# Block inversion of a chunked RWKV-7 layer: its six phases write into the spare half of the chain's bank

## Chip, cores and metric

One Trainium2 chip, one core. The metric is the time of one execution in microseconds of device time; it is given as the median of the runs shown. The profile is of one further execution, taken by the hardware profiler.

## What is computed

Two layers of a decoder on 256 tokens of width 2048 in float32: an RWKV-7 time mixing layer and a differential attention layer, each followed by a gated MLP and layer norms. Only the first layer matters here. Its core is a recurrence over tokens with a 64 x 64 state for each of 32 heads:

```python
def step(S, inp):
    r_t, w_t, k_t, v_t, a_t, b_t = inp
    sa = jnp.einsum('bhij,bhj->bhi', S, a_t)
    S = S * w_t[:, :, None, :] + sa[..., None] * b_t[:, :, None, :] + v_t[..., None] * k_t[:, :, None, :]
    y = jnp.einsum('bhij,bhj->bhi', S, r_t)
    return S, y
...
y = ((y - mean) * lax.rsqrt(var + GN_EPS)).reshape(B, T, D) * lnx_g + lnx_b
...
return (y * g) @ w_o, v_first
```

## The kernel before

Every weight matrix is streamed from HBM, split by ScalarE (`hi`, line 217) and VectorE (`lo`, line 220) into two parts and multiplied in three products; these are the matmuls of lines 230 to 235 into tiles `psd`. They make up most of the kernel.

The recurrence is done in chunks of 64 tokens. The 32 heads are worked in eight groups of four heads (`NG` = 8). `pipeline` (line 1055, in the functions printed below) runs stages i = -3 to 7, and in each stage it traces several generators side by side, by a pace for each: the chain and the outputs of group i, the inversion (`lanes`) of group i + 1, the factors, corners and bonus of group i + 2, the dense products for r and k of group i + 3, and in the last three stages instead of these the first part of the output projection (`early`). The framework then makes each engine's order from this trace, with its own estimate of durations: an instruction that isn't ready is passed by later ones. It also puts in all the waits.

`lanes` inverts, for each of 16 blocks, a triangular 64 x 64 matrix in six phases. A phase is 64 matmuls of 32 x 32 (in the last two 32) into one PSUM tile, then an eviction by VectorE or ScalarE; the next phase needs the evicted values. The matmuls are at lines 1288, 1298, 1311, 1319, 1331 and 1341. The first phase starts from `W1`, which `corners` loads from DRAM, and from its transpose on VectorE (line 1280); the third starts from a transpose of line 1304. In the kernel before each phase takes a new tile from `pst()`: a pool of two banks (`pss`), which the phases share in rotation with the factors (line 1196, evicted into `M` at line 1199), the corners' transposes (line 1255), the bonus and the outputs.

`chain` goes through four chunks. It takes one bank `us` (a pool of one). First all four quarters of it get V centred (line 1374), which is copied into `UV`. From then on only the lower half of the bank is used: `up` (columns 0 to 127, line 1421) and `sp` (columns 128 to 255, line 1434). A chunk is: `rb` (lines 1394 and 1407, other banks), copies into `R`, `up`, copies into `UV` (ScalarE and VectorE), `sp`, the state `Sn` (VectorE, lines 1439 and 1440), and the outputs `yps` (lines 1411 and 1444, other bank). `outputs` normalizes `yps` and writes `V`; from group 4 on `z_parts` splits that into `S1` (lines 197 and 198), which `early` and the output projection multiply with.

The trace order of the chain's 13 steps and the six phases follows from their paces (37.24 and 18.62 with a start at 0.04): phase 1 stands ahead of `up` of chunk 0; phase 2 behind `sp` of chunk 0; phase 3 between `up` and `sp` of chunk 1; phase 4 ahead of `up` of chunk 2; phase 5 behind `sp` of chunk 2; phase 6 behind `up` of chunk 3.

Of the kernel before, what the change touches and what calls it, by code (L numbers as in the profile page):

```python
# [15 lines left out]
T = 256  # L16
# [983 lines left out]
class Groups:  # L1000
# [236 lines left out]
    def corners(self, g):  # L1237
# [31 lines left out]
                                  in_=self.dram(d2, par * 8, ((C, 32), (4 * DBL, 8), (1, 32)), at=be * 2 * DBL))  # L1269
        yield  # L1270

    def lanes(self, g):

        t, nc, g1 = self.t, self.nc, self.g1
        s = self.st[g]
        M, W1, Z = s["M"], s["W1"], self.Z
        rows = [slice(32 * q, 32 * q + 32) for q in range(4)]
        N = [self.units(M, 1)] * 2 + [self.units(M, 0)] * 2
        T0 = g1.tile([P, 8, 32], F32, name="T1")
        nc.vector.transpose(out=T0.rearrange("p u t -> p (u t)"), in_=W1.rearrange("p u t -> p (u t)"))  # L1280
        T0v, W1v = (x.rearrange("p u (b k i) -> p u b k i", b=2, k=2) for x in (T0, W1))
        ps = self.pst()
        pv = ps[:, :P].rearrange("p (u b i) -> p u b i", b=2, i=8)
        with self.ride():
            for u in range(8):
                for q, r in enumerate(rows):
                    be = 32 * (q % 2)
                    nc.tensor.matmul(pv[r, u], lhsT=N[q][r, u, be:be + 32], rhs=T0v[r, u, :, 0, :], start=True, stop=True)
        nc.vector.tensor_tensor(out=self.Z8[:, :, :, 0, :], in0=pv,
                                in1=t.x("m8", 16).rearrange("p (b i) -> p b i", b=2).unsqueeze(1).broadcast_to([P, 8, 2, 8]),  # L1290
                                op=ALU.mult)
        yield
        ps = self.pst()
        pv = ps[:, :P].rearrange("p (u b i) -> p u b i", b=2, i=8)
        with self.ride():
            for u in range(8):
                for r in rows:
                    nc.tensor.matmul(pv[r, u], lhsT=self.Z8[r, u].rearrange("p b k i -> p (b k i)"),
                                     rhs=W1v[r, u, :, 1, :], start=True, stop=True)
        nc.scalar.copy(out=W1v[:, :, :, 1, :], in_=pv)  # L1300
        yield

        T1 = g1.tile([P, 8, 32], F32, name="T1")
        nc.vector.transpose(out=T1.rearrange("p u t -> p (u t)"), in_=W1.rearrange("p u t -> p (u t)"))
        ps = self.pst()
        pv = ps[:, :P].rearrange("p (u t) -> p u t", t=16)
        with self.ride():
            for u in range(8):
                for q, r in enumerate(rows):
                    be = 32 * (q % 2)  # L1310
                    nc.tensor.matmul(pv[r, u, :], lhsT=N[q][r, u, be:be + 32], rhs=T1[r, u, :16], start=True, stop=True)
        self.copy(PACE["ez"][0], Z[:, :, :16], pv)
        yield
        ps = self.pst()
        pv = ps[:, :P].rearrange("p (u t) -> p u t", t=16)
        with self.ride():
            for u in range(8):
                for r in rows:
                    nc.tensor.matmul(pv[r, u, :], lhsT=Z[r, u, :], rhs=W1[r, u, 16:], start=True, stop=True)
        self.copy(PACE["ez"][1], W1[:, :, 16:], pv)  # L1320
        yield

        T2 = g1.tile([P, 8, 32], F32, name="T1")
        nc.vector.transpose(out=T2.rearrange("p u t -> p (u t)"), in_=W1.rearrange("p u t -> p (u t)"))
        Z2 = g1.tile([P, 8, 32], F32, name="T1")
        ps = self.pst()
        pv = ps[:, :T].rearrange("p (u t) -> p u t", t=32)
        with self.ride():
            for u in range(8):
                for q in (0, 2):  # L1330
                    nc.tensor.matmul(pv[rows[q + 1], u, :], lhsT=N[q][rows[q], u, 32:C], rhs=T2[rows[q], u, :],
                                     start=True, stop=True)
        nc.scalar.copy(out=Z2[rows[1]], in_=pv[rows[1]])
        nc.vector.tensor_copy(out=Z2[rows[3]], in_=pv[rows[3]])
        yield
        ps = self.pst()
        pv = ps[:, :T].rearrange("p (u t) -> p u t", t=32)
        with self.ride():
            for u in range(8):
                for q in (0, 2):  # L1340
                    nc.tensor.matmul(pv[rows[q], u, :], lhsT=Z2[rows[q + 1], u, :], rhs=W1[rows[q + 1], u, :],
                                     start=True, stop=True)
        for q in range(4):
            be = 32 * (q % 2)
            o = N[q][rows[q], :, be:be + 32]
            self.copy(PACE["wc"][q], o, W1[rows[q]])
        nc.scalar.copy(out=N[0][rows[0], :, 32:C], in_=pv[rows[0]])
        nc.vector.tensor_copy(out=N[2][rows[2], :, 32:C], in_=pv[rows[2]])
        yield
# [13 lines left out]
    def chain(self, g):  # L1363
# [3 lines left out]
        s = self.st[g]  # L1367
        AR, M, KBT, pc, UV, R = s["AR"], s["M"], s["KBT"], s["pc"], self.UV, self.R
        yps = s["y"] = self.psc.tile([P, GT, T], F32, name="yps")
        us = self.bank("us")  # L1370

        for jj in range(GT):
            for w in range(2):
# [173 lines left out]
```

## Time and profile before

| | us |
|---|---|
| median of the runs | 2480.97 |
| lowest and highest of 3 | 2474.71, 2485.47 |
| the profiled execution | 2477.43 |
| its span in the profile | 2475.7 |
| TensorE busy in the span | 2427.9 (98%) |
| VectorE busy | 1865.6 (75%) |
| ScalarE busy | 1516.3 (61%) |
| mean granted TensorE clock | 0.994 |

A busy engine is one with an instruction in flight, so 98% for TensorE doesn't say that it works at its peak. The stages of `pipeline` lie between about 145 and 560 us of the span; all that follows is attention and MLP, which the change doesn't touch. In the stages the idle time of TensorE, by who released it, tells what the order of the work costs, and the granted clock tells how long a matmul takes.

### The profile page before, as it was taken

To read this page: it belongs to the slowest core of one execution; us is meant where nothing else is said; L and a number is where in the kernel's file an instruction comes from. 1 tells how busy PE (TensorE), PEld (TensorE's weight loads), DVE (VectorE), ACT (ScalarE), POOL (GpSimd) and SP (SyncE) were. 2 spreads that over 40 slices of the span, in tenths; PEclk is the share of its full clock that TensorE was granted. 3 is DMA by queue.
4 is the path that set the end of the run, shared out by engine and by line. 5 is a ranking of instruction groups with operands and counts; after the bars stand their busy time and mean duration, and the time that the engine had idled before them with its cause. 6 is when DMAs were issued, how large, how long until landed. Compare 5 with 4: busy or idle time off the path is not lost.

```text
span 2475.7 us, 53133 instructions
## 1 busy us (share of the span) xinstructions
PE 2427.9 (98%) x18618; PEld 2160.6 (87%) x18618; DVE 1865.6 (75%) x4218; ACT 1516.3 (61%) x3447; POOL 144.5 (6%) x204
## 2 busy tenths in 40 slices
PE   8999999999999999999999999999999999999997
PEld 7988888877988888888889899988988888888886
DVE  8977788868977777776666867678987777776665
ACT  7756675646766666655555756656766666665554
POOL 0010000002200000001111000003200000001111
PEclk9999999999999999999999999999999999999999
DMA  7544443435566666667665555556566666666663
GB/s 244 186 129 120 116 114 115 135 102 159 161 201 188 192 188 190 188 191 226 188 187 160 182 173 166 177 172 181 168 202 190 190 189 189 189 191 184 190 188 121
DMA packets 276717, 428.49 MB, mean 173 GB/s; under 512 B 60632, under 2 KB 83168, under 8 KB 276448
## 3 DMA queue, kind: packets, MB, share of 16 engines
q1 hardware_dynamic: 276448, 425.10, 58.1%
q8 instruction: 145, 2.38, 0.4%
q14 instruction: 124, 1.02, 0.2%
HBM read 420.25 MB, written 6.31 MB: 172 GB/s over the span
## 4 chain that ended last, share of the span: by engine, by line
PE 87%; DVE 6%; ACT 3%; DMA 2%; issue 1%; SPq 0%; POOL 0%; ACTq 0%; DVEq 0%; POOLq 0%
PE psd L234 44%; PE psd L235 22%; PE psd L230 3%; PE psd L232 3%; PE psd L231 3%; DVE lo L220 2%; PE psd L285 1%; PE psd L283 1%; PE psd L284 1%; DMA raw<-in_rkv 1%; PE psd L937 1%; PE psd L936 1%; PE psd L938 1%; ACT hi L217 1%; PE lnst L348 1%
## 5 line engine op out<-in xcount | busy, mean ns | idle before, releaser
L217 ACT CAST hi<-raw 128x256 fp32r<-128x256 f32 (+3 forms) x2236 | 1079.0, 489 | 757.0 <-PE psd L234 542.6
L220 DVE TENSOR_TENSOR lo<-raw,hi 128x256 fp32r<-128x256 f32 (+3 forms) x2236 | 1150.3, 540 | 490.6 <-ACT hi L217 440.2
L234 PE MATMUL psd<-S,hi 128*128 128x512 f32 x2976 | 1040.2, 394 | 0.4 <-ACT hi L217 0.2
L235 PE MATMUL psd<-S,lo 128*128 128x256 f32 x2976 | 832.2, 280 | 0.3 <-DVE lo L220 0.2
L234 PEld LDWEIGHTS psd<-S,hi 128*128 128x128 f32 x2976 | 559.2, 188 | 128.1 <-ACT hi L217 1.0
L235 PEld LDWEIGHTS psd<-S,lo 128*128 128x128 f32 x2976 | 559.2, 188 | 1.7 <-DVE lo L220 1.5
L234 PE MATMUL psd<-hs,hi 128*128 128x512 f32 x1290 | 451.9, 395 | 0.0
L235 PE MATMUL psd<-hs,lo 128*128 128x256 f32 x1290 | 361.3, 280 | 0.0
L234 PEld LDWEIGHTS psd<-hs,hi 128*128 128x128 f32 x1290 | 242.0, 188 | 56.3 <-ACT hi L217 0.6
L235 PEld LDWEIGHTS psd<-hs,lo 128*128 128x128 f32 x1290 | 243.5, 189 | 0.1
L230 PE MATMUL psd<-S,hi 128*128 128x256 f32 x512 | 149.8, 293 | 8.1 <-ACT hi L217 8.1
L232 PE MATMUL psd<-S,lo 128*128 128x256 f32 x512 | 147.5, 288 | 3.1 <-DVE lo L220 3.1
L231 PE MATMUL psd<-S,hi 128*128 128x256 f32 x512 | 146.2, 285 | 0.0
L230 PEld LDWEIGHTS psd<-S,hi 128*128 128x128 f32 x512 | 98.4, 192 | 11.2 <-ACT hi L217 8.1
L234 PE MATMUL psd<-S1r,hi 128*128 128x512 f32 x276 | 105.5, 416 | 2.2 <-issue 1.3
L232 PEld LDWEIGHTS psd<-S,lo 128*128 128x128 f32 x512 | 98.0, 191 | 5.2 <-DVE lo L220 4.2
L231 PEld LDWEIGHTS psd<-S,hi 128*128 128x128 f32 x512 | 98.3, 192 | 1.6 <-issue 1.0
L230 PE MATMUL psd<-S1r,hi 128*128 128x256 f32 x284 | 85.2, 300 | 0.0
L550 DVE SCALAR_TENSOR_TENSOR gc<-gp,cpar,gc 128x256 f32<-128x256 f32 x172 | 83.2, 484 | 2.6
L234 PE MATMUL psd<-S1a,hi 128*128 128x512 f32 x240 | 84.5, 395 | 0.0
L232 PE MATMUL psd<-S1r,lo 128*128 128x256 f32 x284 | 80.8, 285 | 0.3 <-DVE lo L220 0.3
L235 PE MATMUL psd<-S1r,lo 128*128 128x256 f32 x276 | 81.1, 294 | 0.0
(297 smaller groups left out, 3384.2 us busy)
## 6 DMA issues: line engine op xcount, KB each, us to landing
raw<-in_ff_up SPq DMA_DIRECT2D x676, 256.0 KB, 3.8
raw<-in_ff_down SPq DMA_DIRECT2D x320, 256.0 KB, 2.9
raw<-in_rkv SPq DMA_DIRECT2D x192, 256.0 KB, 3.7
raw<-in_da_qk SPq DMA_DIRECT2D x122, 256.0 KB, 3.6
raw<-in_da_v SPq DMA_DIRECT2D x64, 256.0 KB, 3.4
raw<-in_da_o SPq DMA_DIRECT2D x64, 256.0 KB, 3.7
raw<-in_rw_o SPq DMA_DIRECT2D x50, 256.0 KB, 3.5
raw<-in_ff_down SPq DMA_DIRECT2D x32, 192.0 KB, 2.4
```

Of the source, the lines that this page charges most:

```text
L217: nc.scalar.copy(out=hi[:, :s * P], in_=r)
L220: eng.tensor_tensor(out=lo[:, :s * P], in0=r, in1=hi[:, :s * P].bitcast(F32), op=ALU.subtract)
L230: nc.tensor.matmul(ps[:, :T], lhsT=hi, rhs=xs[:, :T], start=first, stop=False)
L231: nc.tensor.matmul(ps[:, :T], lhsT=hi, rhs=xs[:, T:], start=False, stop=False)
L232: nc.tensor.matmul(ps[:, :T], lhsT=lo, rhs=xs[:, :T], start=False, stop=last)
L234: nc.tensor.matmul(ps, lhsT=hi, rhs=xs, start=first, stop=False)
L235: nc.tensor.matmul(ps[:, T:], lhsT=lo, rhs=xs[:, :T], start=False, stop=last)
L283: nc.tensor.matmul(o, lhsT=xh, rhs=hi, start=k == 0 and b == 0, stop=False)
L284: nc.tensor.matmul(o, lhsT=xh, rhs=lo, start=False, stop=False)
L285: nc.tensor.matmul(o, lhsT=xl, rhs=hi, start=False, stop=k == KT - 1 and b == T // P - 1)
L348: self.nc.tensor.matmul(st, lhsT=self.c("onesd"), rhs=t, start=not self.ln_open and n == 0, stop=stop and n == 1)
L550: nc.vector.scalar_tensor_tensor(out=gc, in0=g[:, k:k + T], scalar=cw(k, j), in1=gc, op0=ALU.mult, op1=ALU.add)
```

## The change

The six phases no longer take a tile from `pst()`. They write into the upper half of the bank `us`, columns 256 to 511, by way of `lane()`. In a stage this is the bank which the chain of group i took in the same stage, and `lanes` works on group i + 1. For group 0 there is no chain yet (stage -1): `lanes(0)` takes the bank itself, and `chain(0)` takes it anew after that. Nothing else is changed: the same matmuls, the same evictions, the same paces.

```diff
+    def lane(self):
+        return self.us[:, T:2 * T]
+
     def lanes(self, g):
 
         t, nc, g1 = self.t, self.nc, self.g1
+        if g == 0:
+            self.us = self.bank("us")
...
-        ps = self.pst()
+        ps = self.lane()
         pv = ps[:, :P].rearrange("p (u b i) -> p u b i", b=2, i=8)
...
-        us = self.bank("us")
+        us = self.us = self.bank("us")
```

The line `ps = self.pst()` is replaced in the same way in all six phases.

## Rows read from the trace of the kernel before

**Rows 1.** The page, part 1: busy us, share of the span, instructions.
```profile
PE 2427.9 (98%) x18618; PEld 2160.6 (87%) x18618; DVE 1865.6 (75%) x4218; ACT 1516.3 (61%) x3447; POOL 144.5 (6%) x204
```
**Rows 2.** Busy time by stretch: stretch, its length, engines (instructions), PEclk, DMA share, GB/s.
```profile
255.00:300.00 45.00, 44.83 (x730) 39.86 (x724) 35.53 (x86) 29.07 (x61) 0.98 (x3) 1.00 0.40 114
...
435.00:480.00 45.00, 43.73 (x669) 36.65 (x667) 37.06 (x93) 31.09 (x66) 0.46 (x3) 1.00 0.43 120
...
480.00:525.00 45.00, 43.20 (x708) 33.68 (x710) 28.02 (x75) 20.07 (x47) 0.00 (x0) 0.89 0.44 122
```
**Rows 3.** Waits of TensorE, 165 to 560 us: total us, times, longest.
```profile
PE pss L1331 <- DVE M L1199: 2.4, 3, 1.4
...
PEld pss L1331 <- DVE M L1199: 4.0, 7, 1.6
```
**Rows 4.** Timeline of PE and DVE, stage 2: start, us, engine, line, operation.
```profile
319.94 0.28 DVE L1289 TENSOR_TENSOR Z<-pss,ext 128x128 f32<-128x128 f32 x1
...
320.86 0.27 PE L1421 MATMUL us<-R,M 64*64 64x64 f32 x2
...
328.61 0.45 PE L1434 MATMUL us<-UV,KBT 128*64 128x64 f32 x8
...
330.10 0.44 DVE L1304 STREAM_TRANSPOSE T<-W 128x256 f32<-128x256 f32 x1
...
331.37 0.28 DVE L1440 TENSOR_TENSOR S<-S,pc 128x128 f32<-128x128 f32 x1
...
332.18 0.28 DVE L1103 COPY Z<-pss 128x128 f32<-128x128 f32 x1
...
334.11 0.34 PE L1407 MATMUL b<-S,AR 64*64 64x64 f32 x6
```
**Rows 5.** The same timeline, stage 0.
```profile
229.48 0.27 PE L1421 MATMUL us<-R,M 64*64 64x64 f32 x2
...
230.83 0.45 DVE L1280 STREAM_TRANSPOSE T<-W 128x256 f32<-128x256 f32 x1 [0.28 <-DMA W<-d]
...
233.18 0.28 DVE L1289 TENSOR_TENSOR Z<-pss,ext 128x128 f32<-128x128 f32 x1
```
**Rows 6.** The same timeline, stage 6 and the start of stage 7.
```profile
497.15 0.27 PE L1421 MATMUL us<-R,M 64*64 64x64 f32 x2
...
507.01 0.29 DVE L1289 TENSOR_TENSOR Z<-pss,ext 128x128 f32<-128x128 f32 x1
...
510.17 0.50 PE L234 MATMUL psd<-S1r,hi 128*128 128x512 f32 x1 [1.30 <-issue]
...
516.65 0.70 PE L1434 MATMUL us<-UV,KBT 128*64 128x64 f32 x8
...
525.14 0.45 PE L1444 MATMUL yps<-M,UV 128*64 128x64 f32 x8
...
537.56 0.68 DVE L198 TENSOR_TENSOR S1r<-X,S1r 128x512 fp32r<-128x512 f32 x1
...
539.52 0.42 DVE L1091 TENSOR_TENSOR X<-X,psd 128x256 f32<-128x256 f32 x1
```
**Rows 7.** The same timeline, stage 7, which has no inversion.
```profile
541.00 0.27 PE L1421 MATMUL us<-R,M 64*64 64x64 f32 x2
...
556.37 0.34 PE L1444 MATMUL yps<-M,UV 128*64 128x64 f32 x4
```
**Rows 8.** The same timeline: first matmuls of chain 0, last eviction of `lanes(0)`.
```profile
148.91 0.71 PE L1374 MATMUL us<-ext,X 128*128 128x128 f32 x4 [1.95 <-DVE k L1103]
...
213.53 0.42 DVE L1348 COPY M<-pss 32x256 f32<-32x256 f32 x1
```
**Rows 9.** Busy time by stretch, shorter stretches; columns as in Rows 2.
```profile
145.00:150.00 5.00, 3.05 (x26) 2.85 (x25) 2.44 (x5) 2.58 (x6) 0.26 (x2) 1.00 0.67 219
...
500.00:510.00 10.00, 8.87 (x229) 6.58 (x229) 6.42 (x18) 2.97 (x8) 0.00 (x0) 1.00 0.68 196
...
515.00:520.00 5.00, 5.00 (x57) 3.78 (x55) 3.13 (x9) 1.63 (x4) 0.00 (x0) 0.50 0.11 34
```

More of the change, by code (lines that the diff above doesn't have):

```diff
@@ L1292, in lanes @@
         yield
-        ps = self.pst()
+        ps = self.lane()
         pv = ps[:, :P].rearrange("p (u b i) -> p u b i", b=2, i=8)
@@ L1304, in lanes @@
         nc.vector.transpose(out=T1.rearrange("p u t -> p (u t)"), in_=W1.rearrange("p u t -> p (u t)"))
-        ps = self.pst()
+        ps = self.lane()
         pv = ps[:, :P].rearrange("p (u t) -> p u t", t=16)
@@ L1313, in lanes @@
         yield
-        ps = self.pst()
+        ps = self.lane()
         pv = ps[:, :P].rearrange("p (u t) -> p u t", t=16)
@@ L1325, in lanes @@
         Z2 = g1.tile([P, 8, 32], F32, name="T1")
-        ps = self.pst()
+        ps = self.lane()
         pv = ps[:, :T].rearrange("p (u t) -> p u t", t=32)
@@ L1335, in lanes @@
         yield
-        ps = self.pst()
+        ps = self.lane()
         pv = ps[:, :T].rearrange("p (u t) -> p u t", t=32)
```

## Prediction, made before the changed kernel was run

> **What bounds the kernel now.** I read the page first, then the busy time by stretch over the stages of the pipeline, then TensorE's waits there, then the timelines of three stages. The page shows TensorE busy for 98% of the span [rows 1]: all idle time of TensorE is 2475.7 - 2427.9 = 47.8 us, of which a change inside the stages can reach only the part that lies there. A middle stage takes some 45 us, and TensorE is busy in 44.83 of them [rows 2]: the dense products of group i + 3 fill whatever the chain and the inversion leave open. So a middle stage is bounded by TensorE's own work, which this change doesn't touch, and a chain that gets slower costs nothing as long as there is dense work to put in its place. Only two places differ: the beginning, where TensorE is busy for 3.05 of 5 us at 145 to 150 us [rows 9], and the last stages, with 1.3 us of idle time in 435 to 480, 1.8 us in 480 to 525 and a mean granted clock of 0.89 in the latter [rows 2]. There `early` takes the place of the products, and it needs the results of the chain.
>
> **The change part by part.** The six phases leave the two banks of the pool and enter the chain's bank. No instruction is added or removed; what changes is who waits for whom.
>
> *Removed: the phases' part in the pool's rotation.* A phase now waits for the bank that the factors hold until `M` is evicted: TensorE waited 2.4 us in all for that, three times, always ahead of phase 5 [rows 3]. The weight loads show the same release seven times, 4.0 us, of which most runs beside matmuls still in flight [rows 3]. The matmul row is what TensorE lost: I take -2.4 us; the ends are 0 (the phase meets another wait in the same place) and -4.0.
>
> *Added: one bank for the phases and for `up` and `sp`.* Before, nothing ordered the two against each other. I take it that the framework orders any two accesses in one bank where a matmul writes and another engine reads, so that in trace order each phase must wait until the chain's last read of the bank is over, and the chain's next `up` or `sp` until the phase is evicted. No row of before shows such a wait, since there `up`, `UV`, `sp` and `Sn` follow each other by data anyway; so I work out from the timeline where it would bite. The instruction that waits sits on TensorE's queue, with the dense matmuls behind it; but the order is made with these waits known, so dense matmuls are put ahead of it where there are any.
>
> Phase 1 ahead of `up` of chunk 0: in stage 2 it is evicted at 319.94 + 0.28 = 320.22 us, and `up` starts at 320.86 [rows 4]. No cost. Phase 3 ahead of `sp` of chunk 1: here the order turns round. `sp` ran at 328.61, but phase 3 only after it, because its transpose had to wait for the factors' work on VectorE until 330.10; its eviction ends at 332.18 + 0.28 = 332.46 [rows 4]. So `sp` comes 332.46 - 328.61 = 3.9 us later. But `Sn`, for which `sp` works, was itself late on VectorE: it began its last step at 331.37, and the matmuls that need it went on to 334.11 [rows 4]. With `sp` at 332.5, 0.45 us of it, and two steps of about 0.3 us on VectorE, the state is there at about 334: the chain gets later by some 0 to 1 us. Phases 2, 4 and 5 stand beside `rb` and the copies into `R`, which the chain needs in any case, and phase 6 stands behind the last `up`. So a middle stage: 0 to 1 us more latency of the chain, hidden by the dense products. Cost 0; without that cover it would be up to 3.9 us in each of stages 1 to 5, 19.5 us in all.
>
> In stage 0 and in stage 6 the first phase is late, since `W1` comes late from DRAM: its transpose waits for that DMA in stage 0 [rows 5]. There the eviction ends at 233.18 + 0.28 = 233.5 us where `up` had run at 229.48 [rows 5]: the chain begins 4.0 us later. Products of group 3 stand ready behind it, and TensorE is full there; cost 0, uncovered 4.0. In stage 6 the eviction of phase 1 ends at 507.01 + 0.29 = 507.3, where `up` of chunk 0 had run at 497.15 [rows 6]: the chain of group 6 begins 10.2 us later. This is the dearest place of the change, because what follows is tight: that chain ended at 525.14 + 0.45 = 525.6, `S1` of group 6 was ready at 537.56 + 0.68 = 538.2, and the first product of the last `early`, whose third of four column blocks needs it, was already being added up at 539.52 [rows 6]. Its slack is under a microsecond, and only two banks hold such products, so little can run ahead of it.
>
> How late does the chain of group 6 end? In before it wasn't fast: paced by the trace order, `sp` of chunk 2 came only at 516.65 [rows 6]. An undisturbed chain, from `up` of chunk 0 to the last `yps`, takes 556.37 + 0.34 - 541.00 = 15.7 us in stage 7 [rows 7]. Begun at 507.3 it ends at 523.0 with no phase in between; phase 3 puts its matmuls, its eviction and two hand-overs between `up` and `sp`, some 1.5 us by the durations of rows 4, and each of phases 2, 4 and 5 between 0 and 1 us. That gives 524.5 to 527.5 against 525.6: -1 to +2 us. Steps that are behind their place in the trace go ahead of dense work, so I take the middle, about 0: the dense work that waited behind the chain is done in the 10 us before. Ends: -1 and +10.2 - 1 = +9 (the chain keeps its old distances; one microsecond is the slack).
>
> *Moved: the first matmuls of chain 0.* The eight matmuls of line 1374 for group 0 ran from 148.91 us, where TensorE was idle [rows 8, 9]. They now must follow the last eviction of `lanes(0)`, which ends at 213.53 + 0.42 = 214.0 us [rows 8], into a stretch that is full. Four of them took 0.71 us [rows 8], pipelined behind each other, so eight in a full stretch cost about 1 us: +1.0; ends 0 and +1.4.
>
> *The clock.* In 500 to 510 us, with 229 short matmuls and a wait of 1.30 us at 510.17 [rows 6, 9], TensorE was busy for 8.87 of 10 us, and after that its granted clock was 0.50, the 1.2 GHz level, in 515 to 520 [rows 9]. In 480 to 525 this is (1 - 0.89) x 45 = 5.0 us of clock [rows 2]. The change rearranges just that stretch. It could take the fall away (-5.0) or bring another (+5.0); I take 0, as short matmuls and waits stay in it.
>
> **Sum** against the profiled execution of 2477.43: -2.4 + 0 + 0 + 1.0 + 0 = -1.4, or 2476.0. The median of the runs shown is 3.5 us above the profiled execution, so the median should be about 2479.6, which I round to 2480: no difference that can be measured. About 0.5%, or 12.4 us, is what a measurement of this kernel can tell from no change; the bounds are 2468.6 and 2493.4.
>
> **The rivals**, as medians.
>
> *Forecast*, 0.58: as summed. Own range around 2481: from -4.0 - 1 + 0 = -5.0 to 0 + 2 + 1.4 + 5.0 (one more fall of the clock) = +8.4, so 2476 to 2489.
>
> *The chain of group 6 stays late*, 0.12: the phases' late start in stages 0 and 6 is handed on, because the chain keeps its old distances. It decides from the point at which `S1` of group 6 comes more than 1 us after 538.2. Price 9 in stage 6 and 4.0 in stage 0, with -2.4 and +1.0: +11.6, 2492.6. A little more, such as another fall of the clock, makes it slower by over 0.5%. For it: the slack of under 1 us [rows 6]. Against it: the chain alone needs only 15.7 us [rows 7].
>
> *The chain becomes the bound in all stages*, 0.06: the dense work doesn't cover the 3.9 us of stages 1 to 5. 11.6 + 19.5 = +31, 2512. Against it: 44.83 of 45 us busy [rows 2], and VectorE, the late one, is late either way [rows 4].
>
> *The clock doesn't fall in stage 6*, 0.15: with 10 us of dense work ahead of the late phase 1 the short matmuls and the wait are no longer where they were. -5.0 for the clock, -1.3 for the wait, -2.4 and +1.0: -7.7, 2473.3.
>
> *The change does nothing but free the pool*, 0.09: the halves of the bank are not ordered against each other, and only -2.4 remains, or nothing, 2478.6 to 2481. The Trainium skill speaks against this one: PSUM — Partial Sum Buffer, section "PSUM bank collisions raise a hardware error", says that a matmul's write and another engine's access collide on one bank and the same 32 partitions even at other columns, so that waits have to go by bank and not by address. By that rule the unused half is no place of its own, and the waits of the forecast must be there. No run shown here can tell.
>
> **How the numbers follow.** Likeliest: the forecast, 2480. Faster by over 0.5%: only if the clock and the waits all fall in favour and TensorE's other idle time in the stages goes too, 0.04. Slower: all of the bound in all stages (0.06), half of the late chain (0.06): 0.12. Within: 0.84. The range takes in the clock's case and most of the late chain, and leaves out the chain as the bound in all stages: 2470 to 2493.
>
> **What would show each step.** TensorE's wait of phase 5 for `M` is gone. In stage 6 `up` of chunk 0 starts behind the eviction of phase 1, near 507 us instead of 497; in stage 0 near 233.5; in middle stages `sp` of chunk 1 starts behind the eviction of phase 3. TensorE's busy time in a middle stage stays at 44.8 of 45. `S1` of group 6 is ready within 2 us of 538. The matmuls of line 1374 for group 0 run after 214 us. The prediction is wrong if TensorE shows new waits for evictions of the phases or for copies into `UV` of more than some 5 us in all, if a middle stage gets longer than 45.6 us, or if more or fewer stretches at the lower clock appear.

## The result and the profile after

The changed kernel takes 2474.57 us, the median of 22 runs (2470.76 to 2480.30), against 2477.91 for 22 runs of the kernel before: a ratio of 0.9985 (95% interval 0.9979 to 0.9992). That is a gain of about 3.7 us by the ratio (3.3 us between the medians), within the half per cent of the forecast, which was "no difference that can be measured". The trace shows that it came about in part by another way than the working said.

The lines of the changed kernel lie 5 higher from the second half of `lanes` on: 1311 is 1316, 1331 is 1336, 1374 is 1379, 1421 is 1426, 1434 is 1439, 1444 is 1449. Lines 1154, 1196 and 1199 stay.

Part 1 of the page after, to be held against [rows 1] (span 2472.9 us, before 2475.7):

```profile
PE 2420.0 (98%) x18618; PEld 2153.0 (87%) x18618; DVE 1865.9 (75%) x4218; ACT 1516.0 (61%) x3447; POOL 144.0 (6%) x204
```

One line tells the shape of the result. TensorE runs the same 18618 matmuls in 2427.9 - 2420.0 = 7.9 us **less busy time**, and it is idle for (2472.9 - 2420.0) - (2475.7 - 2427.9) = 52.9 - 47.8 = 5.1 us **more**. The difference of the spans is what remains, 2.8 us. The prediction had it the other way round: 2.4 us less idle time, 1.0 us more work for the first matmuls of chain 0, and TensorE's own work otherwise untouched.

The busy time by stretch after, with the stretches of [rows 2, 9] and three more (columns as in [rows 2]):

```profile
145.00:150.00 5.00, 3.26 (x26) 2.85 (x25) 2.81 (x5) 2.72 (x7) 0.00 (x0) 1.00 0.64 218
150.00:155.00 5.00, 4.79 (x35) 4.13 (x35) 1.61 (x3) 4.98 (x9) 0.66 (x1) 1.00 0.12 38
...
255.00:300.00 45.00, 44.52 (x757) 39.61 (x756) 36.08 (x86) 29.90 (x64) 0.98 (x3) 1.00 0.45 117
435.00:480.00 45.00, 42.05 (x647) 33.82 (x646) 36.86 (x93) 27.73 (x60) 0.98 (x3) 0.96 0.39 110
462.00:464.00 2.00, 0.17 (x6) 0.06 (x5) 2.00 (x6) 0.00 (x0) 0.00 (x0) 1.00 0.00 0
464.00:468.00 4.00, 4.00 (x87) 3.29 (x87) 2.38 (x7) 0.00 (x0) 0.00 (x0) 0.57 0.43 134
480.00:525.00 45.00, 44.36 (x700) 34.52 (x699) 29.95 (x79) 24.61 (x54) 0.00 (x0) 1.00 0.48 134
515.00:520.00 5.00, 5.00 (x86) 3.48 (x85) 2.47 (x8) 1.72 (x6) 0.00 (x0) 1.00 0.17 57
500.00:510.00 10.00, 9.72 (x283) 7.42 (x283) 6.45 (x15) 4.09 (x9) 0.00 (x0) 1.00 0.68 210
532.00:540.00 8.00, 7.69 (x69) 5.65 (x70) 4.14 (x13) 1.50 (x5) 0.00 (x0) 0.57 0.31 84
```

The middle stage keeps 44.52 busy us of 45 but holds 757 matmuls where it held 730: more work is done in the same busy time (a part of that is that the stages stand some 3 us earlier against the window). Stage 6 (480 to 525) is not slowed by the clock in this profile, 1.00 where 0.89 stood, but two stretches at 0.57 have appeared, after 464 and after 532 us.

The waits of TensorE after, 145 to 600 us, to be held against [rows 3] (total us, times, longest):

```profile
PE us L1316 <- DVE T L1309: 1.8, 1, 1.8
PE us L1439 <- DVE UV L1103: 1.6, 7, 0.3
PE us L1426 <- ACT W L1103: 1.6, 3, 1.0
...
PE us L1293 <- DVE UV L1103: 0.9, 2, 0.6
PE us L1293 <- DVE T L1285: 0.6, 1, 0.6
```

The wait of phase 5 for `M` is gone. `up` (L1426) now waits for phase 4's copy `W`, and phase 1 (L1293) for the copies into `UV`, although neither needs the other's values: the order by bank is there.

**Where the time went.** I cut the trace at the first matmul of line 1154 (`kk`, the factors of group 1, 2 and 7) and at the first of line 397, behind the stages; the last stretch ends with the start of TensorE's last matmul. In each stretch, TensorE's gaps are "idle"; half of the time at the lower clock level is "clock" (what a stretch at half speed loses); what is left is "work", busy time as it would be at full clock.

| stretch | before: us (idle, clock, work) | after: us (idle, clock, work) | difference |
|---|---|---|---|
| start to factors of group 1 | 184.2 (15.4, 1.7, 167.1) | 180.8 (13.8, 0, 167.0) | -3.4 |
| to factors of group 2 | 38.4 (2.1, 1.7, 34.6) | 38.6 (1.8, 0, 36.7) | +0.1 |
| to factors of group 7 (five middle stages) | 234.8 (1.6, 0, 233.2) | 231.4 (5.0, 0, 226.4) | -3.4 |
| to the end of the stages | 119.5 (3.4, 5.1, 110.9) | 121.9 (5.5, 5.1, 111.3) | +2.4 |
| all that follows | 1882.5 (9.4, 1.7, 1871.4) | 1883.9 (10.9, 3.4, 1869.7) | +1.5 |

The last line is code that the change doesn't touch; by it one sees how far two executions differ by themselves. The largest single entry is the work in the middle stages, 233.2 - 226.4 = 6.8 us less, of which 5.0 - 1.6 = 3.4 is given back as idle time.

**Where the 6.8 us come from.** The busy time of line 1196 in the middle stages (busy us, mean ns of one matmul), first before, then after:

```profile
L1196 PE MATMUL pss<-AR,KB 64*128 64x128 f32 x160 | 16.7, 285 | 0.0
```
```profile
L1196 PE MATMUL pss<-AR,KB 64*128 64x128 f32 x160 | 11.6, 285 | 0.0
```

The same 160 matmuls, each of the same 285 ns, cover 5.1 us less. That is 5.1 of the 6.8; the other 1.7 us stand on no single row, and kernels in which this line takes the same 16.7 to 16.8 us differ by 1.2 us of work among themselves (233.2 and 232.0, table below). The timeline shows why the line takes less. TensorE in stage 2 before (start, us, line):

```profile
330.72 0.72 PE L1311 MATMUL pss<-T,M 32*32 32x16 f32 x64
331.37 0.38 PE L232 MATMUL psd<-S,lo 128*128 128x256 f32 x1
331.69 1.16 PE L1196 MATMUL pss<-AR,KB 64*128 64x128 f32 x8
332.77 0.33 PE L1407 MATMUL b<-S,AR 64*64 64x64 f32 x2
333.02 1.16 PE L1196 MATMUL pss<-AR,KB 64*128 64x128 f32 x8
...
339.70 1.16 PE L1196 MATMUL pss<-AR,KB 64*128 64x128 f32 x16
```

The same place after:

```profile
326.34 0.71 PE L1316 MATMUL us<-T,M 32*32 32x16 f32 x64
...
327.40 0.29 DVE L1103 COPY Z<-us 128x128 f32<-128x128 f32 x1
...
327.76 0.45 PE L1439 MATMUL us<-UV,KBT 128*64 128x64 f32 x8
328.05 0.40 PE L1449 MATMUL yps<-M,UV 128*64 128x64 f32 x8
...
328.38 1.16 PE L1196 MATMUL pss<-AR,KB 64*128 64x128 f32 x16
```

Line 1196 multiplies two heads in turn. One lies on partitions 0 to 63, the other on 64 to 127, and each has its own bank from the pool. Issued in turn, all sixteen take 1.16 us, as long as the eight of one head alone (1.16 us): the two heads' matmuls run at the same time. Line 1196 works on a group in two halves; in the kernel before the second half shows this too (339.70, `x16`). In the first half before, phase 3 (L1311) held one of the pool's two banks; so the first head's eight were put ahead, and the other head's followed when phase 3 was evicted, for another 1.16 us. TensorE had other work in between, so no row of waits tells of it. The Trainium skill has both facts, which I had not brought together: TensorEngine Tiling (Array Packing), section "Key Properties", says that different tiles of the array can multiply in parallel, and section "Gotcha 1: PSUM Pressure" that row tiles need different banks; the trace agrees with the first (1.16 us for 16), and nothing here tests the second.

### The profile page after: what moved, and what is told of

Read it like the earlier page. It is cut to its first block, busy times and chain, and to the rows that moved or that the text cites. A ratio compares the mean times of both kernels' runs of the same rounds, so it can differ in the third digit from the quotient of the medians.

```text
span 2472.9 us, 53169 instructions
## 1 busy us (share of the span) xinstructions
PE 2420.0 (98%) x18618; PEld 2153.0 (87%) x18618; DVE 1865.9 (75%) x4218; ACT 1516.0 (61%) x3447; POOL 144.0 (6%) x204
## 4 chain that ended last, share of the span: by engine, by line
PE 83%; DVE 9%; DMA 4%; ACT 2%; issue 2%; SPq 0%; ACTq 0%; POOL 0%; DVEq 0%; POOLq 0%
PE psd L234 43%; PE psd L235 22%; DVE lo L220 3%; PE psd L230 3%; PE psd L232 3%; PE psd L231 3%; PE psd L285 1%; PE psd L283 1%; PE psd L284 1%; DMA raw<-in_rkv 1%; ACT hi L217 1%; DMA raw<-in_rw_o 1%; PE psd L937 1%; PE psd L936 1%; PE psd L938 1%
```

## The experiments

All ratios are against the kernel before; in the experiments on the same chip, under "before" in the row. The last two columns come from one profile of each kernel.

| kernel | us | before | ratio (95%) | middle stages: idle, clock, work | L1196 there |
|---|---|---|---|---|---|
| before (profile) | | | | 1.6, 0, 233.2 | 16.7 |
| changed (profile) | 2474.57 | 2477.91 | 0.9985 (0.9979 to 0.9992) | 5.0, 0, 226.4 | 11.6 |
| group 0 only | 2475.59 | 2476.96 | 1.0000 (0.9990 to 1.0010) | 2.7, 3.2, 232.0 | 16.8 |
| groups 1 to 7 only | 2476.00 | 2476.96 | 0.9994 (0.9981 to 1.0007) | 5.3, 0, 227.2 | 11.6 |
| before, chain 0 held back | 2479.43 | 2476.96 | 1.0011 (1.0002 to 1.0020) | 3.6, 0, 232.0 | 16.7 |
| changed, heads apart | 2474.96 | 2476.96 | 0.9997 (0.9986 to 1.0009) | 1.7, 0, 231.8 | 17.1 |
| before, heads in turn | 2478.88 | 2475.26 | 1.0012 (1.0000 to 1.0023) | 2.8, 0, 231.0 | 14.0 |
| changed, not in the last group | 2471.67 | 2475.26 | 0.9988 (0.9979 to 0.9998) | 5.0, 0, 226.2 | 11.6 |
| changed, phases later | 2477.00 | 2475.26 | 1.0008 (0.9999 to 1.0018) | 8.2, 3.4, 226.5 | 12.5 |
| phase 3 only | 2473.24 | 2477.94 | 0.9982 (0.9970 to 0.9994) | 4.5, 0, 226.8 | 11.6 |
| phases 3 and 5 only | 2473.83 | 2477.94 | 0.9981 (0.9972 to 0.9990) | 6.2, 1.7, 225.4 | 11.6 |
| changed, again | 2475.04 | 2477.94 | 0.9991 (0.9980 to 1.0003) | 5.9, 0, 226.2 | 11.6 |
| not in the last group, again | 2474.55 | 2477.94 | 0.9987 (0.9979 to 0.9996) | 4.7, 0, 226.1 | 11.6 |

Read the last two columns first. Wherever line 1196 takes 11.6 us, the work of the middle stages is 225.4 to 227.2; wherever it takes 16.7 to 17.1, it is 231.8 to 233.2. Of the two between, 12.5 goes with 226.5 and 14.0 with 231.0.

**The two parts of the change by themselves.** First, the spare half for group 0 alone, and then for all other groups alone (there `lanes(0)` takes no bank ahead of the chain). In both the six calls pass `g`.

```diff
-    def lane(self):
-        return self.us[:, T:2 * T]
+    def lane(self, g):
+        return self.us[:, T:2 * T] if g == 0 else self.pst()
```

> Only the inversion of group 0 writes to the spare half of the bank; groups 1 to 7 keep the pool of two banks. Theory A (the gain of the change is made in the middle stages, where the factors' matmuls of line 1196 get both banks of the pool at once): no gain of the middle stages, the first half of line 1196 keeps taking 2.5 us instead of 1.16 in groups 3 to 6. Theory B (the gain is made at the beginning, where the first matmuls of chain 0 no longer hold TensorE up and the granted clock no longer falls twice): the whole 3.3 us that the changed kernel was ahead at the start of chain 0, about 2474.5 against 2478, ratio 0.9987. If both hold, this kernel shows B's 3.3 us and none of the new waits of later stages.

```diff
+    def lane(self, g):
+        return self.us[:, T:2 * T] if g else self.pst()
...
-        if g == 0:
-            self.us = self.bank("us")
```

> Groups 1 to 7 write to the spare half, group 0 keeps the pool and chain 0 takes its bank at the old place. Theory A: line 1196 takes 1.16 us a half in groups 2 to 7, stages 0 to 5 together are about 3.4 us shorter than before, ratio about 0.9987 or better by the 2.4 us that the last stages may give back either way. Theory B: the beginning is as before, a wait of about 2 us ahead of the first matmuls of chain 0 at 147 to 149 us and two stretches at half clock; and if B alone were the cause, ratio 1.000.

With group 0 alone the middle stages stay as before (232.0, row 16.8), and the factors of group 1 come at 181.6 us, as in the changed kernel (180.8), not at 184.2. With the other groups alone it is the reverse: 227.2 in the middle, and a start like before (185.9). So the two parts act in different places and don't need each other. Neither by itself can be told from no change by its ratio, and for the first the expected 0.9987 is ruled out (1.0000, with an interval from 0.9990): what it gains at the start is lost again by the factors of group 7, which come at 459.3 us against 457.5. Its clock falls at 149.3 us as before, so its gain at the start isn't the clock's. The start of the second, by stretch, answers to [rows 9]:

```profile
145.00:150.00 5.00, 2.74 (x24) 2.54 (x23) 1.37 (x3) 1.70 (x5) 0.84 (x5) 1.00 0.73 213
150.00:155.00 5.00, 5.00 (x24) 4.43 (x25) 1.44 (x3) 3.26 (x6) 0.00 (x0) 0.66 0.25 79
183.00:188.00 5.00, 3.47 (x11) 2.47 (x11) 4.94 (x15) 4.89 (x8) 0.00 (x0) 0.66 0.42 151
```

With chain 0's first matmuls still at 150 us, one wait of 2.26 us stands ahead of them, the clock falls just behind it, and again after 183 us.

**Only the place of chain 0's first matmuls.** In the kernel before they are held until the inversion of group 0 is done, with all phases in the pool; `mm` is the last matmul of phase 6.

```diff
+        self.inv = mm.ins
...
+        with t.tc.issue_after(self.inv) if g == 0 else nullcontext():
             for jj in range(GT):
                 for w in range(2):
```

> The kernel before, with one thing changed: the first matmuls of chain 0 are put behind the last matmul of the inversion of group 0. Theory B: the wait of 1.95 us at 147 us splits up or goes, the clock doesn't fall at 150 and 184 us, and the kernel is 2 to 3.4 us faster, ratio about 0.9988. Rival: the beginning is faster because the inversion of group 0 no longer shares the pool (phase 5 waited 1.43 us there); then this kernel is like before, ratio 1.000.

The expected gain (0.9988) did not come; by its ratio the kernel is slightly slower than before. The start does gain what it gains in the changed kernel: the factors of group 1 come at 181.3 us. But the next stretch, to the factors of group 2, takes 44.6 us, against 38.4 before, since the clock falls twice in it and loses 5.1 us there (stretches by columns as before; the seventh figure is the clock):

```profile
195.00:200.00 5.00, 5.00 (x130) 4.82 (x118) 4.40 (x10) 1.77 (x5) 0.00 (x0) 0.66 0.02 5
208.00:217.00 9.00, 9.00 (x85) 8.67 (x79) 3.86 (x7) 4.09 (x8) 0.00 (x0) 0.62 0.53 134
```

Shortly ahead of the second stretch, phase 5 of group 0 waits 1.41 us for `M` in the pool. The middle stages are those of before (232.0, row 16.7): moving the chain's first matmuls has nothing to do with the gain there.

**The heads of line 1196 apart, in the changed kernel.** The loop over heads is put outside.

```diff
-                for n, c in enumerate((0, 2, 1, 3) if jj == 0 else (1, 3, 0, 2)):
-                    uu = jj * NC + c
-                    for h, ps in enumerate(banks):
+                for h, ps in enumerate(banks):
+                    for n, c in enumerate((0, 2, 1, 3) if jj == 0 else (1, 3, 0, 2)):
+                        uu = jj * NC + c
```

> The changed kernel, with the matmuls of line 1196 issued for one pair of heads (one half of the rows) after the other instead of in turn. Theory A says that in turn they run side by side on the two halves of the rows: apart, 16 rows take about 2.3 us instead of 1.16, which is 1.1 us for each of the 16 halves, 14 of them in full stages: 15 us or more, ratio about 1.006 against the changed kernel, 1.005 against before. Rival (the turn doesn't matter, only when a bank is free): 1.16 us as before and no change against the changed kernel, ratio 0.9985 against before.

```profile
331.90 1.71 PE L1196 MATMUL pss<-AR,KB 64*128 64x128 f32 x16
...
338.20 1.71 PE L1196 MATMUL pss<-AR,KB 64*128 64x128 f32 x16
```

Sixteen matmuls take 1.71 us and not the 2.3 expected: one head right behind the other, they still overlap at the seam (the eight of each alone would be 1.16). But now both halves of a group are slow, and the line takes 17.1 us. The work in the middle goes from 226.4 to 231.8, +5.4, against +5.5 on the line itself. So the excess of work in the kernel before is, in the main, the lost pairing. But the expected ratio of 1.005 against before failed, and by far (0.9997): the idle time falls back to 1.7 us, and by its ratio the kernel can't be told from either of the two. At full clock, idle time and work together, the middle stages take 233.5 us, against 231.4 in the changed kernel: of the 5.4 us that pairing saves, 3.3 were spent in waiting.

**The heads in turn, in the kernel before.** Each matmul of line 1196 is put behind the one ahead of it.

```diff
+            mm = None
...
-                        nc.tensor.matmul(ps[:, n * P:(n + 1) * P], lhsT=KB[hr, uu, :, :], rhs=AR[hr, uu, :, :],
-                                         start=True, stop=True)
+                        with nullcontext() if mm is None else t.tc.issue_after(mm.ins):
+                            mm = nc.tensor.matmul(ps[:, n * P:(n + 1) * P], lhsT=KB[hr, uu, :, :],
+                                                  rhs=AR[hr, uu, :, :], start=True, stop=True)
```

> The kernel before with its pool shared as it was, and one thing added: each matmul of line 1196 is queued behind the one before it, so that the two heads of a pair must go in turn. Theory A (matmuls of the two halves of the rows start almost together when they go in turn, and the pool's shortage of a bank had pulled them apart): 1.16 us for 16 rows in every group, 6.5 us less work of TensorE than before, of which a wait for the second bank may give back some: span less clock loss about 2455 to 2458 against 2460, ratio about 0.998. Rival (the time of the stages is set elsewhere, what line 1196 saves is given back as waits): span less clock loss 2460, ratio 1.000.

```profile
335.49 0.73 PE L1313 MATMUL pss<-T,M 32*32 32x16 f32 x64
336.46 0.48 PE L1198 MATMUL pss<-AR,KB 64*128 64x128 f32 x2
337.81 1.16 PE L1198 MATMUL pss<-AR,KB 64*128 64x128 f32 x14
```

This missed. Two matmuls start while phase 3 (here L1313) still holds the other bank, the other fourteen come after its eviction, and the half group is spread over 2.51 us as before. So the heads didn't go strictly in turn either: the two that start first lie 0.21 us apart, as two of one head do, where those of different heads start within 0.01 us. The line falls only to 14.0 us, the work in the middle to 231.0, and the kernel isn't faster. This order didn't make up for the missing bank; one that keeps them strictly in turn wasn't run.

**The last group in the pool, as before.** The one stage whose slack was under a microsecond [rows 6] is taken out of the change.

```diff
+    def lane(self, g):
+        return self.us[:, T:2 * T] if g < NG - 1 else self.pst()
```

> The changed kernel, but the inversion of group 7 keeps the pool, so that the chain of group 6 no longer waits for its late first phase. If that wait is what the last stages gave back (2.4 us between the factors of group 7 and the end of the stages): up of chunk 0 near 494 us instead of 503, and 2 us or so faster than the changed kernel, ratio about 0.9975 against before. Rival (the dense work covers it, the last stages lost their time to the clock and to S1): no difference to the changed kernel, ratio 0.9985 to 0.999.

`up` of chunk 0 in stage 6 starts at 492.70 us:

```profile
492.70 0.27 PE L1426 MATMUL us<-R,M 64*64 64x64 f32 x2
```

That is 10.6 us ahead of the changed kernel (503.25), with the factors of group 7 at 450.8 us in both, so the late start there is due to the order by bank. The last stages take 118.2 us from the factors of group 7 in one profile and 120.8 in the other, against 121.9 and 125.9 for the two of the changed kernel; 3.7 and 5.0 us less, and in either pair the clock alone makes 5.1 (0 against 5.1 lost, 1.7 against 6.8). By the ratios (0.9988 and 0.9987 against 0.9985 and 0.9991) the two kernels are the same, as the rival had it; the expected 0.9975 didn't come. (For a hint that the two do differ, see what stays open.)

**The phases a little later.** With another start, phases 4 and 6 shift against the chain's steps.

```diff
-            lanes0=0.04, early0=0, products0=0,
+            lanes0=0.06, early0=0, products0=0,
```

> The changed kernel with the phases started at 0.06 instead of 0.04, so that in trace order phase 1 stands behind up of chunk 0 and phase 3 behind sp of chunk 1. If the new waits come from the turned order (sp behind phase 3, up behind phase 1), these are gone: the chain of group 6 starts near 494 us, TensorE's waits for line 1316 and ahead of up shrink, span less clock loss 2 to 3 us under the 2460.5 of the changed kernel. Rival: the waits move to other pairs of phase and chain, no difference.

```profile
PE us L1324 <- DVE UV L1103: 6.7, 6, 1.9
```

This row is of 145 to 600 us; 6.3 us of it lie in the middle stages. Line 1324 is phase 4. It now stands behind `up` of chunk 2 and waits for the copies into `UV`, which read the other half of the bank. The turned order is gone, as expected: phase 3 (L1316) has no wait left, and `up` of chunk 0 in stage 6 starts at 496.61 us. But the waits moved to this other pair, which was the rival. The timeline of one such wait:

```profile
286.34 0.28 DVE L1103 COPY Z<-us 128x128 f32<-128x128 f32 x1
...
292.68 0.28 DVE L1103 COPY UV<-us 64x128 f32<-64x128 f32 x1 [0.83 <-ACT UV L1103]
...
293.02 0.73 PE L1324 MATMUL us<-W,Z 32*32 32x16 f32 x64 [1.91 <-DVE UV L1103]
```

Its own input `Z` was there at 286.62, 6.4 us before it began. So this wait is of the bank alone. Idle time in the middle rises from 5.0 to 8.2 us, and the gain is used up: what the order by bank costs depends on the place of each phase among the chain's steps, and the start of 0.04 is the better one of the two.

**Which phase does it?** For groups 1 to 6 only phase 3, and then only phases 3 and 5, go into the spare half; group 0 goes there wholly, group 7 stays in the pool. The calls pass `g` and the number of the phase; the second kernel has `(3, 5)` in place of `(3,)`.

```diff
+    def lane(self, g, n):
+        return self.us[:, T:2 * T] if g == 0 or g < NG - 1 and n in (3,) else self.pst()
```

> Groups 1 to 6 put only phase 3, the one that held a bank when the first half of line 1196 came, into the spare half of the chain's bank; their other phases and all of group 7 keep the pool, group 0 is as in the changed kernel. Theory A (the working time that the change saves in the middle stages is the pairing of line 1196, and it is phase 3 that stood in its way): TensorE's busy time at full clock from the factors of group 2 to those of group 7 falls to about 226.5 us as with all phases moved, against 232 to 233 with all in the pool; with fewer ordered pairs the idle time there is 2 to 4 us instead of 5. Rival (the other phases take the bank in its place): 231 to 233.

> As the one with phase 3 alone, with phase 5 moved too, which waited for the second half's bank: work about 226.5 us in the same stretch, and the wait ahead of phase 5 for the eviction into M gone; idle time no more than with phase 3 alone if that wait was real, more if the new order behind sp of chunk 2 costs as much.

```profile
328.43 0.45 PE L1439 MATMUL us<-UV,KBT 128*64 128x64 f32 x8
329.04 1.16 PE L1196 MATMUL pss<-AR,KB 64*128 64x128 f32 x16
331.61 0.73 PE L1324 MATMUL pss<-W,Z 32*32 32x16 f32 x64 [0.35 <-DVE M L1199]
```

These are from the first of the two. Phase 3 alone restores the pairing (11.6 us, work 226.8), with 4.5 us of idle time where 2 to 4 were expected; the other five phases bring nothing of it. Phase 4 in the pool now waits for `M`, 0.35 us here and 1.7 us in the five stages. With phases 3 and 5 it is the same work within 1.4 us and a little more idle time (6.2 against 4.5 us), though the wait of phase 5 for `M` is gone. Both kernels are as fast as the changed one or slightly faster (0.9982 and 0.9981, with 0.9991 for the changed kernel beside them); their intervals overlap, so I don't call either better.

**The changed kernel and the one without the last group, again,** for comparison with those two:

> The changed kernel once more, beside the others on one chip: ratio about 0.9985 against before if its gain is its own, 0.999 to 1.000 if it is of the size of the scatter between chips and profiles.

> The kernel that leaves group 7 in the pool, once more beside the changed kernel: if the late first phase of group 7 costs, 2 to 4 us faster than the changed kernel in the same call; if only its clock differed by chance, the same within 1.5 us.

Their medians lie 0.5 us apart, so the 2 to 4 us that a costly first phase of group 7 would have brought didn't come. They repeat the middle stages within 0.3 us of work (226.2 and 226.1) and within 0.9 us of idle time. The changed kernel's profile this time has a span of 2478.9 us, 6.0 above its first, with seven stretches at half clock ahead of the idle end of TensorE, where the first has three; one begins at 151.2 us and one, of 6.8 us, at 513.0, just where the kernel before had them and the first profile had none. The interval of this second comparison takes in no change (0.9980 to 1.0003). Single profiles of one kernel differ by more than what is asked about.

## Why the prediction was right, and where its working was not

**The bound.** "Bounded by TensorE's own work, which this change doesn't touch" was half right. The stages are bounded by that work, and so a chain that is late costs little. But the change did touch it: where a matmul stands among others decides how much of it is covered. The first halves of line 1196 start 45.6 us apart before (286.1, 331.7, 377.3, 422.9) and 44.8 to 45.2 after (283.2, 328.4, 373.3, 418.1). The work of the middle stages stood at 0 and measured -6.8 us in this pair of profiles, 5.1 of it on line 1196; it is the step that failed. It could have been seen in the trace before: the first half of a group showed as two rows of `x8` with 1.16 us each (331.69 and 333.02), the second half as one row of `x16` with 1.16 (339.70).

**Removed: the pool's waits, -2.4.** The wait of phase 5 for `M` is gone, as forecast. But only 0.4 of it lay in the middle stages, 2.0 us elsewhere, and other waits came in the same stretches.

**Added: the order by bank, 0.** Mis-sized. The turned order came as described: after, phase 3 is evicted at 327.69 and `sp` of chunk 1 follows at 327.76. It was right, too, that TensorE does other work meanwhile. But it doesn't do so everywhere: in the middle stages waits for `UV` at L1439 and L1293 and for `W` at L1426 make 1.3 + 0.9 + 1.2 = 3.4 us, against 0.2 us for `UV` and 0.4 us for `M` in the kernel before. Only the last two, 2.1 us, are of the bank alone; L1439 is `sp`, which multiplies `UV`, and waits for its own input. Over 145 to 600 us these lines make 1.6 + 0.9 + 1.6 = 4.1 us, and with 0.8 us of `rb` (L1399) for `UV` 4.9: just under the 5 us at which I would have called the forecast wrong (the 1.8 us of phase 3 for its own transpose, L1316, not counted). The middle stages didn't get longer either. But another of the signs named did appear: ahead of TensorE's idle end the clock falls three times, and four times before.

**Stage 0, 0 and uncovered 4.0.** Rows of the changed kernel that answer to [rows 5]:

```profile
227.53 0.44 DVE L1285 STREAM_TRANSPOSE T<-W 128x256 f32<-128x256 f32 x1
...
229.06 0.28 DVE L1294 TENSOR_TENSOR Z<-us,ext 128x128 f32<-128x128 f32 x1
229.68 0.27 PE L1426 MATMUL us<-R,M 64*64 64x64 f32 x2
```

`up` does follow the eviction of phase 1 (229.34). It starts at 229.68 and not at 233.5, mostly because all of this comes 3.3 us earlier than in the kernel before; against the factors of group 2 (222.7, then 219.4) it is 3.5 us later, near the 4.0 that were worked out. The only wait of TensorE beside it is one of 0.26 us.

**Stage 6, 0 (ends -1 and +9).** Rows that answer to [rows 6]:

```profile
502.65 0.28 DVE L1294 TENSOR_TENSOR Z<-us,ext 128x128 f32<-128x128 f32 x1
503.25 0.27 PE L1426 MATMUL us<-R,M 64*64 64x64 f32 x2
...
515.66 0.45 PE L1439 MATMUL us<-UV,KBT 128*64 128x64 f32 x8
...
521.29 0.34 PE L1449 MATMUL yps<-M,UV 128*64 128x64 f32 x4
...
532.02 0.69 DVE L198 TENSOR_TENSOR S1r<-X,S1r 128x512 fp32r<-128x512 f32 x1
```

The chain starts behind phase 1, 6.1 us later than before, and ends at 521.6, 4.0 us earlier. `S1` is ready at 532.7 against 538.2. But the stage itself came 6.7 us earlier (factors of group 7 at 457.5, then 450.8); measured from there the chain starts 12.8 us later, where 10.2 was worked out, ends 2.7 us later and has `S1` ready 1.1 us later. It caught up on most of its delay, to a little over the sum's -1 to +2, and the rival in which it keeps its distances didn't come. The last stages cost +2.4 in this pair of profiles, where 0 was put down.

**Moved: chain 0's first matmuls, +1.0.** They stand where the forecast put them, past 214 us:

```profile
217.42 0.38 PE L1379 MATMUL us<-ext,X 128*128 128x128 f32 x2
218.73 0.83 PE L1379 MATMUL us<-ext,X 128*128 128x128 f32 x6
```

The work from the factors of group 1 to those of group 2 grows by 36.7 - 34.6 = 2.1 us, and by 1.9 to 2.4 in all kernels that move them or hold them back. The term was too small by a factor of two. (In the kernel before six of the eight stood at 149 us; the other two came at 185.87.) The other half of the move was missing: at 148.91 those matmuls stood behind a wait of 1.95 us [rows 8], with dense matmuls held behind them. After, at that place:

```profile
147.32 0.39 PE L230 MATMUL psd<-mid,l 128*128 128x256 f32 x1 [0.89 <-ACT l L865]
...
148.68 0.39 PE L232 MATMUL psd<-mid,l 128*128 128x256 f32 x1 [0.85 <-DVE l L867]
```

Two short waits in place of one long one, and in 150 to 155 us a clock of 1.00. The start gains 3.4 us in this pair, 1.6 of idle time and 1.7 of clock. The part of the clock doesn't repeat: of the ten profiles with these matmuls moved or held back, five have a fall at 149.3 to 151.2 us all the same, the second one of the changed kernel among them. The gain of the start is there in every kernel with these matmuls moved (factors of group 1 at 180.7 to 183.9 us, 178.8 to 181.3 with the clock taken out) against 184.2 to 186.2 (182.5 to 184.2) in those without.

**The clock, 0 with ends of 5.0.** In the first profile the fall of stage 6 that was costed at 5.0 us is gone (1.00 in 480 to 525), as the fourth rival had it; but 1.7 us of clock came back behind the wait at 462 us and 3.4 after 532, so that the last stages lose 5.1 in both. The forecast's zero was right there by luck, by two changes that cancel; in the second profile of the changed kernel a fall at 513.0 us is back, and the last stages lose 6.8. Not costed were the two falls at the start (150 and 184 us, 1.7 us each), which the first profile after doesn't have.

**The rival that the halves aren't ordered** is out: phase 4 waiting 1.91 us for the copies out of the other half shows it. The rule of the Trainium skill, PSUM — Partial Sum Buffer, section "PSUM bank collisions raise a hardware error", asks for waits by bank and not by address; the waits agree with it. That two accesses would collide without them no run here shows.

**The sum.** The forecast had -1.4: -2.4 of idle time and +1.0 of work. Measured in the pair of profiles: -6.1 of work, -1.7 of clock and +5.1 of idle time, -2.7 by these rounded terms, beside a difference of the spans of -2.8. The code behind the stages, which the change doesn't touch, has its scatter in this: to the end of the stages alone it is -4.4 of work, -3.4 of clock and +3.6 of idle time, -4.2 in all. The size came out near, the terms didn't, so the nearness was luck: work that the sum left out and waits that it put at 0 nearly cancel. The 2480 itself rested on a median of three runs, 2480.97, which lies 3.1 us above that of the 22; so 2474.57 lies outside the forecast's own range of 2476 to 2489, while the movement of -3.3 lies inside its -5.0 to +8.4.

**What stays open.** Taking out the clock from the span of every run by its mean granted clock (to three digits, and with the stretch at the end where TensorE has no work), the kernel before needs 2459.3 to 2461.1 us in the three comparisons and the changed one 2460.5 and 2460.6; the clock takes 14.1 to 15.1 us from the one and 12.4 and 13.4 from the other. By this, the 0.15% is mostly clock; but the changed kernel's second set stands beside 2461.1 on its own chip, and the first has no such partner. By the single profiles, some 1 us of the 2.8 is work and idle time together, and the rest clock. The two readings agree that in the changed kernel the structure gives back nearly all of the 6.8 us; whether a microsecond of it stays can't be told.

The same reckoning hints at more where group 7 keeps the pool. The four such sets need 2456.1 (without the last group), 2458.9 (again), 2458.6 (phase 3 only) and 2456.3 us (phases 3 and 5), which is 3.1, 2.2, 2.5 and 4.8 us less than the kernel before beside them, with standard errors of 0.6 to 0.7; the changed kernel beside the last three is 0.5 us less. The profiles don't show where it would come from: with the clock taken out, the time to the end of the stages is 567.0 to 568.2 us in these four, 567.6 in both profiles of the changed kernel and 568.4 in the one before. So this is open too.

## What to carry to other kernels

Before calling a full engine's work fixed, look at how its small matmuls are packed: a group that shows the same busy time for `x8` as elsewhere for `x16` is running without the partner that would go beside it. A scarce bank costs in two ways, by waits, which the profile lists, and by pulling apart work that would run side by side, which it lists nowhere. Where a freed bank serves one such place, move only what blocks it: phase 3 alone brought the whole saving of work here. And work that is saved is not yet time that is saved: here most of it came back as waits.

## What the runs showed of the hardware that was not expected

Two streams of 64-row matmuls on the two halves of the partitions, issued in turn to two banks, start in pairs within 0.01 us and take 1.16 us for 16, where eight of one stream alone take 1.16 as well; 16 issued one head behind the other take 1.71; pulled apart they take two times 1.16.

The clock fell to its lower level (1.2 GHz) behind waits of TensorE: in the kernel before behind 1.95 us (a wait from 147.0), 2.03 (181.3), 1.31 (508.9) and 2.78 (606.7); after the change behind 1.83 (462.1), behind 0.80 and 0.61 (529.7 and 531.4), and behind 2.78 (602.5). But a wait is not enough: with the phases shifted, the wait of 1.91 us that ends at 293.02 is followed by a full clock, as is, in the kernel without the last group, a wait of 1.83 us that ends at 464.03, the same wait of phase 3 that a fall follows in the changed kernel; and with group 0 alone in the spare half a fall at 425.8 us has no wait of over 0.5 us ahead of it. What else decides was not settled. Such a stretch lasted 3.4, 6.8 or 10.2 us in these two profiles and cost 1.7 to 5.1 us, so that a change worth under 3 us can't be read from single profiles.
